# An encoder block in split float32r: branch projections as split products, S5 states turned back before the read-out

## The chip, the cores and the metric

The kernel runs on one core of a Trainium2 chip. The metric is the device time of one execution in microseconds; three timed runs of the kernel before gave 1187.72, 1187.76 and 1188.9, and the median counts. A profiled execution of the same program gives the trace.

## The reference

Two layers over a residual stream x of 256 tokens by 1024 features, all in float32:

```
for l in range(2):
    x = x + 0.5 * swiglu_ffn(rmsnorm(x), ffn1_w_up[l], ffn1_w_down[l])      # hidden width 2816
    h = rmsnorm(x)
    u, q, k, v, z, gates = split(h @ w_in[l])                               # 256, 512, 512, 512, 512, 3072
    y_s5   = GLU(gelu(S5(u)), s5_w_glu[l]) @ w_br_s5[l]     # 16 groups of 16 channels, 64 complex states each
    y_attn = chunked_attention(q, k, v) @ w_br_attn[l]      # 8 heads of 64, chunks of 64
    y_conv = silu(layernorm(conv31(glu(z)))) @ w_br_conv[l] # depthwise, causal, 256 channels
    g = sigmoid(gates + b)
    x = x + (g_s5 * y_s5 + g_attn * y_attn + g_conv * y_conv) @ w_out[l]
    x = x + 0.5 * swiglu_ffn(rmsnorm(x), ffn2_w_up[l], ffn2_w_down[l])
```

S5 is a linear recurrence of complex states, s[t] = a s[t-1] + B u[t] with a = mag e^(i theta), and its output is the real part of C s[t], plus a skip term.

## The kernel before

The residual stream is kept with features on the partitions and 256 tokens along the free dimension, so a weight matrix is used in 128x128 tiles as the stationary operand and a product's moving operand has 256 columns. The tiles come in the order of their use (`PLAN`), eight to a chunk of 512 KB, from one stream of DMAs on SP's queue. For most products (*split* products here) a chunk lands in `raw` (three buffers), ScalarE (ACT) casts it to float32r as `hi`, and VectorE (DVE) subtracts to get the rest, `lo` (four buffers each, in `fetch`). The other operand is split in the same way by `split` (a cast on ACT, a subtraction on DVE), and `prod` adds hi x hi, hi x lo and lo x hi in PSUM: three matmuls.

Three weight matrices of each layer are named in `NATIVE`: `w_br_conv` (16 tiles), `s5_w_glu` (8) and `w_br_s5` (16), five chunks. They land in a `lo` buffer as they are, are not split, and `prod` issues one plain float32 matmul with an operand that isn't split either: the convolution's result `cv`, the GELU's result `gh` (written by `s5_gelu`) and the GLU's result `so` (in buffer `u`).

S5 works in a rotating frame, so that the recurrence becomes a real scan. For each of eight blocks of 128 states, `s5_states` multiplies B u by tables of cos and sin, adds and subtracts, scans twice (real and imaginary part, buffer `sa`), and then multiplies the scans by cos (result `mc`) and by sin (result written over the tables, `tbl`). The four combinations are left apart: for four blocks at a time the read-out on TensorE (PE) adds four products per block, `mc` real and imaginary, `tbl` imaginary and real, with `cc`, which holds C times a coefficient in three forms of sign. These products have a stationary tile of 32 columns, so four sit side by side in the array.

The order of issue is not that of the code. The program is recorded, and a list scheduler (`Recorder.schedule`) runs it with rough prices and puts each engine's instructions in an order that then stands: engines run in order. Among instructions that are ready it takes the lowest rank. The weight stream, products and evacuations have rank 0, the heads of the attention 1, the convolution 2, S5's states and GELU 3, the next layer's S5 tables 4; a matmul of a rank above 0 goes ahead of the others on PE when it is ready. The matrices come in this order: w_in's gates (24 blocks), w_br_attn, four blocks of w_br_conv, s5_w_glu, the other four of w_br_conv, w_br_s5, w_out. The steps of the branches fill in between the gates' products. A block of a branch's projection is multiplied by its gate and added by DVE as it leaves PSUM (two operations for the convolution, two and a split for S5). `w_out` starts with a pair of output blocks that takes its last operand block as late as it can.

Every recorded instruction is issued in one place, so the trace has line 268 for nearly all of them; tiles tell them apart. The prices that the scheduler uses are:

```
return max(n / 2400.0 * (4 * rows / P if slow else 1) + 0.0025, 0.03), 0.2     # PE, n columns
return SLACK * (0.068 + scal + n / (1920.0 if fast else 960.0)), 0.16          # DVE, SLACK = 1.02
```

Of the kernel before, what the change touches and what calls it, by code (L numbers as in the profile page):

```python
"""Two layers of a parallel-branch encoder block (SwiGLU / S5 + attention + conv mixer / SwiGLU).

The residual stream is kept feature-major: x[feature on partitions, feature block, token].
Every large product runs on the tensor engine in float32r: both operands are split exactly
into a high part of 12 significant bits and the remainder, and three products carry the sum.
RMSNorm's 1/rms factor is per token and linear, so it is applied where a product leaves PSUM.
"""
# [10 lines left out]
F32 = mybir.dt.float32  # L18
# [11 lines left out]
CW = 31  # L30
U0, Q0, K0, V0, Z0, G0 = 0, 2, 6, 10, 14, 18     # 128-column blocks of w_in
CHT = 8                                            # weight tiles per DMA
MAGIC = 12582912.0                                 # 1.5 * 2**23: adding it rounds to integers
TWO_PI = 6.283185307179586
C1 = float(np.float32(6.28125))                    # 2*pi in three parts
# [13 lines left out]
GLU = 4                                            # blocks of the convolution's branch ahead of S5's GLU  # L49


def plan():
    out = []
    for l in range(L):
        for f in ("ffn1", "ffn2"):
# [5 lines left out]
            # the last operand block as late as possible  # L61
# [17 lines left out]
NATIVE = ("w_br_conv", "s5_w_glu", "w_br_s5")      # few columns: float32 products, operands not split  # L79
# [20 lines left out]
#  # L100
# The program is first recorded in its logical order. Each engine runs its instructions in the order
# of issue, so that order is then chosen by a list scheduler with rough costs (they depend on shapes
# alone): the weight stream and what frees PSUM go first, the mixer's branches fill in.
# [23 lines left out]
class Recorder:  # L127
# [65 lines left out]
    def price(eng, name, outs, ins, kw):  # L193
# [5 lines left out]
        if eng == "pe":  # L199
            if name == "transpose":  # L200
                return 0.112, 0.2
            slow = kw["rhs"].dtype != F32R or n < 256
            rows = outs[0].partition_size()            # tiles of 32 or 64 columns run side by side
            return max(n / 2400.0 * (4 * rows / P if slow else 1) + 0.0025, 0.03), 0.2
# [12 lines left out]
    def schedule(self):  # L217
# [4 lines left out]
        wait = {e: [] for e in engs}       # (ready time, seq, op)  # L222
        can = {e: [] for e in engs}        # (rank, seq, op)
# [6 lines left out]
        while left:  # L230
# [11 lines left out]
            if soon:                       # a short chain that others wait for: no long one in between  # L242
                free[e] = min(soon)
                continue
# [26 lines left out]
# blocks of x that are loaded ahead of a part (chunk, column) of the weights  # L271
# [8 lines left out]
class Builder:  # L280
# [15 lines left out]
    # -- small helpers --  # L296
# [4 lines left out]
    # Tiles of one tag take turns in their slots, so work that runs at its own pace has its own tags.  # L301
# [15 lines left out]
    # -- weight stream --  # L317
    def fetch(self, upto):
        nc = self.nc
        while self.fetched <= min(upto, NCH - 1):  # L320
            c = self.fetched
            n = min(CHT, len(PLAN) - c * CHT) * P
            if PLAN[c * CHT][1] in NATIVE:
                raw = self.tile(self.chunk, [P, CHT * P], F32, "lo", 4)
                nc.sync.dma_start(out=raw, in_=self.w_d[c])
                self.chunks[c] = (raw, None)
                self.fetched += 1
                continue
# [14 lines left out]
    def wt(self, key, n=1):  # L343
        i = INDEX[key]
        c, o = divmod(i, CHT)
        self.fetch(c + 2)
        hi, lo = self.chunks[c]
        s = slice(o * P, (o + n) * P)
        return hi[:, s], None if lo is None else lo[:, s]

    # -- products: out[feature, token] += w.T @ x --
    def prod(self, out, keys, ops, ks, start, stop):
        nc = self.nc
        for n, k in enumerate(ks):
            wh, wl = self.wt(keys(k))
            if wl is None:
                nc.tensor.matmul(out, lhsT=wh, rhs=ops[:, k, :], start=start and n == 0,
                                 stop=stop and n == len(ks) - 1)
                continue
            if not isinstance(ops, tuple):  # L360
                # one pass over both parts; the halves of out are added where it leaves PSUM
# [18 lines left out]
    def quad(self, outs, l, name, cs, ops, nk):  # L380
        """Output blocks that share every operand block as it arrives."""
        for k in range(nk):
            for o, c in zip(outs, cs):
                self.block(o, l, name, c, ops, nk, k, k + 1)

    def pair(self, outs, l, name, cs, ops, nk):
        """Two output blocks whose last operand block is used as late as possible."""
# [5 lines left out]
    # -- 1/sqrt on a small tile: bit-level seed and three Newton steps --  # L393
# [12 lines left out]
    def col_rsqrt(self, terms, inv_n, eps=EPS):  # L406
        """terms: [feature, token] tiles whose squares' sums over all features give the variance."""
# [10 lines left out]
    def spread(self, rc, out):  # L418
        """out[:, token] = rc[token] on every partition."""
# [9 lines left out]
    # -- RMSNorm: operands x*g split in two, 1/rms per token --  # L429
# [33 lines left out]
    # -- SwiGLU half step --  # L463
# [58 lines left out]
    # -- S5: decay and rotation tables --  # L522
# [23 lines left out]
    def s5_tables(self, l):  # L546
        """Returns a list of steps: cos/sin(theta*s) for every state and s, decay, and C times coef."""
# [7 lines left out]
        def small_part():  # L555
# [4 lines left out]
            # B, for products of split operands stacked along the contraction: rows (hi, hi, lo)  # L560
# [35 lines left out]
        def angle(j):  # L596
            # fraction of a turn in [-1/2, 1/2]
# [21 lines left out]
        def coefs():  # L619
# [17 lines left out]
            # C times coef, with the signs under which the four products of a state add up  # L637
            c4 = st["ct"].rearrange("p (j r c) -> p j r c", j=8, r=2)
            cc = self.tile(self.res, [P, 8, 3, 32], F32, "cc")
# [5 lines left out]
            ts(out=cc[:, :, 1, :], in0=cc[:, :, 0, :], scalar1=-1.0, scalar2=None, op0=ALU.mult)  # L645
            tt(out=cc[:, :, 2, :], in0=c4[:, :, 0, :], in1=b(ci), op=ALU.mult)
            tt(out=t2, in0=c4[:, :, 1, :], in1=b(cr), op=ALU.mult)
            stt(out=cc[:, :, 2, :], in0=cc[:, :, 2, :], scalar=-1.0, in1=t2, op0=ALU.mult, op1=ALU.subtract)
# [5 lines left out]
    # -- mixer --  # L654
    def mixer(self, l, after):
# [6 lines left out]
        # u  # L662
# [12 lines left out]
        # S5 states, two groups (128 states) at a time  # L675
        y_ps = {}

        def s5_states(j):
            if j % 4 == 0:
                # channels of one state block on the same partitions, parts (hi, lo, hi) stacked  # L680
# [27 lines left out]
            # the products with sin take the place of this block's tables  # L708
            mc = self.tmp("mc", 2 * T)
            tt(out=v3(mc), in0=v3(z), in1=b3(cosj), op=ALU.mult)  # L710
            tt(out=tab, in0=v3(z), in1=b3(sinj), op=ALU.mult)
            mcs.append(mc)
            if j % 4 == 3:
# [4 lines left out]
                for n, (w, i) in enumerate(((0, 0), (2, 1), (1, 1), (2, 0))):  # L718
                    for q in range(4):
                        jj = 4 * b + q  # L720
                        rhs = (mcs[jj][:, i * T:(i + 1) * T] if n < 2 else st["tab"][:, jj, i, :])
                        nc.tensor.matmul(y_ps[0][32 * q:32 * q + 32, b * T:(b + 1) * T], lhsT=cc[:, jj, w, :], rhs=rhs,
                                         start=n == 0, stop=n == 3, tile_position=(0, 32 * q))
# [4 lines left out]
        def s5_gelu(b):  # L728
            # gelu(y) (tanh form), doubled
# [8 lines left out]
            if not ge:  # L738
                ge["y"] = self.tile(self.big, [P, 2, T], F32, "gh")
            stt(out=ge["y"][:, b, :], in0=t, scalar=1.0, in1=y, op0=ALU.add, op1=ALU.mult)  # L740

        # conv: GLU with both halves of z
# [13 lines left out]
        # q, k, v with tokens on partitions  # L756
# [23 lines left out]
        # operands of the gates: normalised, in place  # L780
# [5 lines left out]
        # twice the convolution (hp holds twice the GLU): LayerNorm takes that out, with four times EPS  # L786
# [3 lines left out]
        cv = self.tile(self.big, [P, 2, T], F32, "cv")  # L790

# [11 lines left out]
        def conv_norm():  # L803
# [17 lines left out]
            for q in range(2):  # L821
                # silu(v), doubled: v*(1 + tanh(v/2))
# [4 lines left out]
                stt(out=cv[:, q, :], in0=th, scalar=1.0, in1=v, op0=ALU.add, op1=ALU.mult)  # L827
# [71 lines left out]
        # gates, with the branches' steps in between  # L899
# [19 lines left out]
        # branches' projections, gated and added  # L919
# [5 lines left out]
        def conv_block(j):  # L925
            ps = self.bank(("mm", "at", "mm", "at", "mm")[j % 5])
            self.block(ps[:, :T], l, "w_br_conv", j, cv, 2)
# [6 lines left out]
        so = self.tile(self.big, [P, 2, T], F32, "u")  # L934
        for b in range(2):
# [5 lines left out]
            stt(out=so[:, b, :], in0=t, scalar=1.0, in1=ps[:, :T], op0=ALU.add, op1=ALU.mult)  # L941
# [30 lines left out]
    def warm_up(self):  # L972
        """While the first loads are under way: the tensor engine's clock up, the Tanh table in."""
# [11 lines left out]
    def build(self):  # L985
        nc = self.nc
        # small parameters of the first layer and x come as one array
# [33 lines left out]
def layout(inputs):  # L1021
# [8 lines left out]
    sb = np.zeros((L, 3, 2, 16, 8, 2, 2, 64), np.float32)      # copy, g, ch | jb, re/im, g, state  # L1030
    for l in range(L):
# [19 lines left out]
        ct = np.zeros((2, 64, 8, 2, 2, 16), np.float32)        # g, state | jb, re/im, g, ch  # L1051
# [7 lines left out]
    # relative position bias per head, blocks (q 0..127, k 0..127) and (q 128..255, k 0..255);  # L1059
    # keys of later chunks are masked  # L1060
# [3 lines left out]
    full = inp["attn_rel_bias"][:, :, rel]                     # L, heads, q, k  # L1064
# [29 lines left out]
```

## Time and profile before

| | us |
|---|---|
| timed runs, median (three runs) | 1187.76 (1187.72 to 1188.9) |
| profiled execution: span from the first to the last instruction | 1186.6 |
| what the runs' median has on top of that span | 1.2 |
| PE busy | 1177.4 |
| PE weight loads (beside PE) | 1097.8 |
| DVE busy | 927.2 |
| ACT busy | 645.6 |

The profiled execution is given by its span; no time of its own from outside is listed beside it, so the runs' median stands for it. Busy is the union of an engine's instructions. A matmul's record is longer than the distance to the next, since matmuls overlap; that distance, from start to start, is called pitch below, and it is what a product costs on a full PE. The granted clock of PE is full (1.000 of 2.4 GHz) over the whole span.

### The profile page before, as it was taken

The page shows a single profiled execution, that of the slowest core. Times are in us where ns is not written, and L with a number is a line of the kernel's source. Part 1 is how long each engine was busy: PE and PEld are TensorE (multiplying, and loading weights), DVE is VectorE, ACT ScalarE, POOL GpSimd, SP SyncE. Part 2 cuts the span into 40 slices and gives each one's busy share as a digit, 9 for nine tenths or more (in the row PEclk, how much of TensorE's full clock was granted, in tenths as well). Part 3 has the DMA queues.
Part 4 walks back from the last instruction along what each step waited for, and adds up shares of the span by engine and source line. Part 5 has one row for each costly group of instructions (what it writes and reads, how often), then busy time and mean ns, then how long its engine had stood idle before and what let it go on. Part 6 is the DMA issues. An engine that isn't in the chain of part 4 may idle for free.

```text
span 1186.6 us, 21932 instructions
## 1 busy us (share of the span) xinstructions
PE 1177.4 (99%) x8565; PEld 1097.8 (93%) x8565; DVE 927.2 (78%) x1898; ACT 645.6 (54%) x1171; POOL 13.0 (1%) x32
## 2 busy tenths in 40 slices
PE   8999999999999999999999999999999999999998
PEld 7999989898888999998899999898987999999987
DVE  7999876998789998766676666779987888666654
ACT  6546554787643546645544444557875435444442
POOL 0000000000200000000000000000001000000000
PEclk9999999999999999999999999999999999999999
DMA  7655556554334565555555555565533435555552
GB/s 253 212 181 187 195 182 226 195 178 146 101 131 162 178 196 187 187 178 191 182 178 186 187 179 190 184 213 198 192 126 94 152 126 194 194 179 182 189 198 89
DMA packets 59751, 209.97 MB, mean 177 GB/s; under 512 B 6912, under 2 KB 9088, under 8 KB 59392
## 3 DMA queue, kind: packets, MB, share of 16 engines
q1 hardware_dynamic: 58496, 207.79, 50.9%
q8 instruction: 67, 1.10, 0.4%
q0 software_dynamic: 1152, 0.79, 0.3%
q14 instruction: 36, 0.29, 0.1%
HBM read 206.72 MB, written 1.05 MB: 175 GB/s over the span
## 4 chain that ended last, share of the span: by engine, by line
PE 98%; DMA 1%; DVE 0%; ACT 0%; SPq 0%; issue 0%; DVEq 0%
PE mm L268 72%; PE at L268 22%; PE ax L268 2%; PE y L268 1%; DMA px<-in_x 1%; PE pq L268 0%; SPq L268 0%; DVE x L268 0%; DVE acc L268 0%; ACT sq L268 0%; DVE lo L268 0%; DVE ev L268 0%; ACT x L268 0%; DVE px L268 0%; ACT ev L268 0%
## 5 line engine op out<-in xcount | busy, mean ns | idle before, releaser
L268 ACT CAST hi<-raw 128x1024 fp32r<-128x1024 f32 (+1 forms) x373 | 389.8, 1047 | 406.8 <-issue 166.7
L268 DVE TENSOR_TENSOR lo<-raw,hi 128x1024 fp32r<-128x1024 f32 (+1 forms) x373 | 454.9, 1221 | 165.7 <-ACT hi L268 161.9
L268 PE MATMUL mm<-x,hi 128*128 128x256 f32 x2736 | 505.8, 284 | 1.9 <-ACT hi L268 1.8
L268 PEld LDWEIGHTS mm<-x,hi 128*128 128x128 f32 x2736 | 424.5, 189 | 11.4 <-issue 7.4
L268 PE MATMUL mm<-x,lo 128*128 128x256 f32 x1368 | 388.3, 285 | 0.4 <-DVE lo L268 0.2
L268 PEld LDWEIGHTS mm<-x,lo 128*128 128x128 f32 x1368 | 257.2, 188 | 4.7 <-issue 3.8
L268 PE MATMUL mm<-AB,hi 128*128 128x512 f32 x704 | 246.6, 398 | 0.0
L268 PE MATMUL mm<-AB,lo 128*128 128x256 f32 x704 | 193.1, 281 | 0.0
L268 PE MATMUL at<-x,hi 128*128 128x256 f32 x1040 | 188.6, 282 | 0.1
L268 PEld LDWEIGHTS at<-x,hi 128*128 128x128 f32 x1040 | 160.6, 189 | 0.3 <-ACT hi L268 0.3
L268 PEld LDWEIGHTS mm<-AB,hi 128*128 128x128 f32 x704 | 130.6, 188 | 29.7
L268 PE MATMUL at<-x,lo 128*128 128x256 f32 x520 | 146.6, 282 | 0.0
L268 PEld LDWEIGHTS mm<-AB,lo 128*128 128x128 f32 x704 | 132.9, 189 | 2.6
L268 PEld LDWEIGHTS at<-x,lo 128*128 128x128 f32 x520 | 97.9, 188 | 0.0
L268 PE MATMUL mm<-tbl,hi 128*128 128x256 f32 x256 | 46.3, 284 | 0.0
L268 PE MATMUL at<-hi,x 128*128 128x512 f32 x128 | 41.0, 396 | 0.0
L268 PEld LDWEIGHTS mm<-tbl,hi 128*128 128x128 f32 x256 | 39.9, 192 | 0.3 <-ACT tbl L268 0.3
L268 ACT ACTIVATE th<-ev 128x256 f32<-128x256 f32 x88 | 36.2, 412 | 7.2 <-DVE ev L268 7.0
L268 ACT CAST AB<-ev 128x256 fp32r<-128x256 f32 x88 | 34.9, 400 | 6.5 <-DVE ev L268 6.2
L268 DVE SCALAR_TENSOR_TENSOR ev<-th,ev 128x256 f32<-128x256 f32 x88 | 36.8, 419 | 1.2 <-ACT th L268 1.2
L268 DVE TENSOR_TENSOR AB<-ev,AB 128x256 fp32r<-128x256 f32 x88 | 36.6, 419 | 0.4 <-ACT AB L268 0.2
L268 DVE TENSOR_TENSOR ev<-mm,rb 128x256 f32<-128x256 f32 x56 | 23.6, 424 | 15.6 <-PE mm L268 13.5
(222 smaller groups left out, 1174.1 us busy)
## 6 DMA issues: line engine op xcount, KB each, us to landing
raw<-in_w SPq DMA_DIRECT2D x371, 512.0 KB, 3.7
lo<-in_w SPq DMA_DIRECT2D x10, 512.0 KB, 4.4
AB<-in_b SPq DMA_DIRECT2D x2, 1536.0 KB, 7.9
mc<-in_s SPq DMA_DIRECT2D x8, 192.0 KB, 4.1
out_x<-px SPq DMA_DIRECT2D x8, 128.0 KB, 3.2
raw<-in_w SPq DMA_DIRECT2D x2, 256.0 KB, 3.8
px<-in_x SPq DMA_DIRECT2D x1, 512.0 KB, 7.7
ct<-in_p SPq DMA_DIRECT2D x2, 256.0 KB, 3.7
```

Of the source, the lines that this page charges most:

```text
L268: fn(*args, **kw)
```

## The change

The three matrices of `NATIVE` go through the same way as all others: their chunks land in `raw`, are cast and split, and the products have three float32r matmuls. Their operands are split where they are written: the convolution's result into `cv2`, which takes the buffers of `ct` and `hp`; the GELU's into the buffers `gh` and `gl`; the GLU's into the buffer `us`. And in S5 two more operations per block (`mc` real minus `tbl` imaginary, `mc` imaginary plus `tbl` real) turn the states back, so that the read-out has two products per block in place of four and `cc` two forms in place of three. Comments that go are left out here.

```diff
-NATIVE = ("w_br_conv", "s5_w_glu", "w_br_s5")      # few columns: float32 products, operands not split
 def fetch(self, upto):
...
-            if PLAN[c * CHT][1] in NATIVE:
-                raw = self.tile(self.chunk, [P, CHT * P], F32, "lo", 4)
-                nc.sync.dma_start(out=raw, in_=self.w_d[c])
-                self.chunks[c] = (raw, None)
-                self.fetched += 1
-                continue
 def prod(self, out, keys, ops, ks, start, stop):
...
-            if wl is None:
-                nc.tensor.matmul(out, lhsT=wh, rhs=ops[:, k, :], start=start and n == 0,
-                                 stop=stop and n == len(ks) - 1)
-                continue
 # s5_tables, coefs
-            cc = self.tile(self.res, [P, 8, 3, 32], F32, "cc")
+            cc = self.tile(self.res, [P, 8, 2, 32], F32, "cc")
-            ts(out=cc[:, :, 1, :], in0=cc[:, :, 0, :], scalar1=-1.0, scalar2=None, op0=ALU.mult)
 # s5_states
             tt(out=v3(mc), in0=v3(z), in1=b3(cosj), op=ALU.mult)
             tt(out=tab, in0=v3(z), in1=b3(sinj), op=ALU.mult)
+            tt(out=mc[:, :T], in0=mc[:, :T], in1=tab[:, 1, :], op=ALU.subtract)
+            tt(out=mc[:, T:], in0=mc[:, T:], in1=tab[:, 0, :], op=ALU.add)
...
-                for n, (w, i) in enumerate(((0, 0), (2, 1), (1, 1), (2, 0))):
+                for r in range(2):
                     for q in range(4):
                         jj = 4 * b + q
-                        rhs = (mcs[jj][:, i * T:(i + 1) * T] if n < 2 else st["tab"][:, jj, i, :])
-                        nc.tensor.matmul(y_ps[0][32 * q:32 * q + 32, b * T:(b + 1) * T], lhsT=cc[:, jj, w, :], rhs=rhs,
-                                         start=n == 0, stop=n == 3, tile_position=(0, 32 * q))
+                        nc.tensor.matmul(y_ps[0][32 * q:32 * q + 32, b * T:(b + 1) * T], lhsT=cc[:, jj, r, :],
+                                         rhs=mcs[jj][:, r * T:(r + 1) * T], start=r == 0, stop=r == 1,
+                                         tile_position=(0, 32 * q))
 # s5_gelu
-                ge["y"] = self.tile(self.big, [P, 2, T], F32, "gh")
-            stt(out=ge["y"][:, b, :], in0=t, scalar=1.0, in1=y, op0=ALU.add, op1=ALU.mult)
+                ge["y"] = tuple(self.tile(self.big, [P, 2, T], F32R, g) for g in ("gh", "gl"))
+            stt(out=t, in0=t, scalar=1.0, in1=y, op0=ALU.add, op1=ALU.mult)
+            self.split(t, ge["y"][0][:, b, :], ge["y"][1][:, b, :])
 # mixer
+        cv2 = (self.tile(self.big, [P, 2, T], F32R, "ct"), self.tile(self.big, [P, 2, CW - 1 + T], F32R, "hp")[:, :, :T])
 # conv_norm
-                stt(out=cv[:, q, :], in0=th, scalar=1.0, in1=v, op0=ALU.add, op1=ALU.mult)
+                stt(out=v, in0=th, scalar=1.0, in1=v, op0=ALU.add, op1=ALU.mult)
+                self.split(v, cv2[0][:, q, :], cv2[1][:, q, :])
 # conv_block
-            self.block(ps[:, :T], l, "w_br_conv", j, cv, 2)
+            self.block(ps[:, :T], l, "w_br_conv", j, cv2, 2)
 # mixer, S5's GLU
-        so = self.tile(self.big, [P, 2, T], F32, "u")
+        so = self.tile(self.big, [P, 2, 2, T], F32R, "us")
+        so = (so[:, 0, :, :], so[:, 1, :, :])
...
-            stt(out=so[:, b, :], in0=t, scalar=1.0, in1=ps[:, :T], op0=ALU.add, op1=ALU.mult)
+            stt(out=t, in0=t, scalar=1.0, in1=ps[:, :T], op0=ALU.add, op1=ALU.mult)
+            self.split(t, so[0][:, b, :], so[1][:, b, :])
```

## Rows read from the trace of the kernel before

**Rows 1.** The page, part 1: busy us (share of the span) xinstructions of each engine.

```profile
PE 1177.4 (99%) x8565; PEld 1097.8 (93%) x8565; DVE 927.2 (78%) x1898; ACT 645.6 (54%) x1171; POOL 13.0 (1%) x32
```

**Rows 2.** The page, part 4: the chain that ended last, by engine.

```profile
PE 98%; DMA 1%; DVE 0%; ACT 0%; SPq 0%; issue 0%; DVEq 0%
```

**Rows 3.** Windows: length, busy us of each engine, clock, DMA share, GB/s, of six stretches.

```profile
251.50:351.70 100.20, 100.20 (x761) 88.34 (x760) 85.08 (x202) 64.22 (x158) 5.96 (x12) 1.00 0.39 131
351.70:369.60 17.90, 17.90 (x144) 16.32 (x144) 14.65 (x38) 9.60 (x16) 0.00 (x0) 1.00 0.65 218
369.60:383.10 13.50, 13.50 (x64) 11.64 (x62) 13.31 (x31) 3.44 (x7) 0.00 (x0) 1.00 0.35 119
383.10:389.60 6.50, 6.50 (x55) 6.50 (x55) 6.50 (x16) 1.55 (x4) 0.00 (x0) 1.00 0.21 79
837.20:937.60 100.40, 100.40 (x760) 88.39 (x759) 84.83 (x198) 64.43 (x158) 5.81 (x12) 1.00 0.38 131
937.60:952.90 15.30, 15.30 (x134) 14.04 (x133) 12.68 (x34) 7.42 (x12) 0.00 (x0) 1.00 0.51 172
```

**Rows 4.** Chain in order of time, FFN1 of layer 0: start us, us, what.

```profile
33.75 17.28 PE mm L268 x144
```

**Rows 5.** Timeline of PE, projections of layer 0: start us, us, engine, instruction, count.

```profile
365.73 1.03 PE L268 MATMUL mm<-cv,lo 128*128 128x256 f32 x4
...
369.18 3.62 PE L268 MATMUL mm<-gh,lo 128*128 128x256 f32 x16
372.64 1.89 PE L268 MATMUL mm<-cv,lo 128*128 128x256 f32 x8
```

**Rows 6.** Timeline of PE around one single read-out product, layer 0.

```profile
341.42 0.27 PE L268 MATMUL mm<-x,hi 128*128 128x256 f32 x1
341.63 0.62 PE L268 MATMUL y<-mc,cc 128*32 128x256 f32 x2
...
342.40 0.28 PE L268 MATMUL mm<-x,lo 128*128 128x256 f32 x1
```

**Rows 7.** Timeline of PE around the second group of read-out products, layer 0.

```profile
361.89 0.28 PE L268 MATMUL mm<-nat,hi 128*128 128x256 f32 x1
362.10 0.83 PE L268 MATMUL y<-mc,cc 128*32 128x256 f32 x9
...
362.78 1.24 PE L268 MATMUL y<-tbl,cc 128*32 128x256 f32 x13
...
364.17 0.28 PE L268 MATMUL mm<-nat,lo 128*128 128x256 f32 x1
```

**Rows 8.** Timeline of DVE, layer 0, behind the GLU and in the first output pair.

```profile
373.91 0.42 DVE L268 SCALAR_TENSOR_TENSOR u<-ev,mm 128x256 f32<-128x256 f32 x1
...
388.00 1.22 DVE L268 TENSOR_TENSOR lo<-raw,hi 128x1024 fp32r<-128x1024 f32 x1
389.14 0.42 DVE L268 TENSOR_TENSOR tbl<-ev,tbl 128x256 fp32r<-128x256 f32 x1
389.47 0.35 DVE L268 TENSOR_SCALAR sa<-iota,fh 128x256 f32<-128x256 f32 x1
```

**Rows 9.** Waits of DVE in the gates of layer 0: us, times, longest.

```profile
DVE lo L268 <- ACT hi L268: 7.0, 12, 1.4
```

**Rows 10.** Timeline of DVE around the GELU's last write, layer 0, then layer 1.

```profile
366.79 0.42 DVE L268 SCALAR_TENSOR_TENSOR ev<-AB,mm 128x256 f32<-128x256 f32 x1 [0.24 <-PE mm L268]
...
369.14 0.42 DVE L268 SCALAR_TENSOR_TENSOR gh<-sc,sa 128x256 f32<-128x256 f32 x1
369.47 0.42 DVE L268 SCALAR_TENSOR_TENSOR AB<-ev,AB 128x256 f32<-128x256 f32 x1
...
952.45 0.43 DVE L268 SCALAR_TENSOR_TENSOR gh<-sc,sa 128x256 f32<-128x256 f32 x1
952.86 0.42 DVE L268 SCALAR_TENSOR_TENSOR ev<-AB,mm 128x256 f32<-128x256 f32 x1
```

**Rows 11.** The page, part 6: DMA issues, count, KB each, us to landing.

```profile
raw<-in_w SPq DMA_DIRECT2D x371, 512.0 KB, 3.7
```

More of the change, by code (lines that the diff above doesn't have):

```diff
@@ L348, in wt @@
         s = slice(o * P, (o + n) * P)
-        return hi[:, s], None if lo is None else lo[:, s]
+        return hi[:, s], lo[:, s]
     def prod(self, out, keys, ops, ks, start, stop):
@@ L644, in coefs @@
             tt(out=cc[:, :, 0, :], in0=cc[:, :, 0, :], in1=t2, op=ALU.subtract)
-            ts(out=cc[:, :, 1, :], in0=cc[:, :, 0, :], scalar1=-1.0, scalar2=None, op0=ALU.mult)
-            tt(out=cc[:, :, 2, :], in0=c4[:, :, 0, :], in1=b(ci), op=ALU.mult)
+            tt(out=cc[:, :, 1, :], in0=c4[:, :, 0, :], in1=b(ci), op=ALU.mult)
             tt(out=t2, in0=c4[:, :, 1, :], in1=b(cr), op=ALU.mult)
-            stt(out=cc[:, :, 2, :], in0=cc[:, :, 2, :], scalar=-1.0, in1=t2, op0=ALU.mult, op1=ALU.subtract)
+            stt(out=cc[:, :, 1, :], in0=cc[:, :, 1, :], scalar=-1.0, in1=t2, op0=ALU.mult, op1=ALU.subtract)
             st["cc"] = cc
```

## The prediction

> **What bounds the kernel now.** I read the page first, then the chain, then the stages, then single instructions. The page shows TensorE (PE) busy for 1177.4 of 1186.6 us [rows 1], and the chain that ended last is PE for 98% [rows 2]. Where PE never stops, the time is the sum of the pitches (start to start) of its matmuls, so a cheaper product would be worth its whole saving. But that is a mean over stages. The table by stage [rows 3] has one line for each stretch around the change: the gates with S5, heads and convolution in between (251.5 to 351.7 and 837.2 to 937.6), the start of the attention projection up to the write of S5's GELU (351.7 to 369.6, 937.6 to 952.9), the rest of the projections (369.6 to 383.1) and the first output pair. PE is busy all through, and VectorE (DVE) is 85% busy in the gates (85.08 of 100.20), 82 and 83% ahead of the GELU, 99% behind it (13.31 of 13.50), 100% after that. So in the second half of the mixer DVE has almost nothing to spare, and the first question is whether PE or DVE sets the end there.
>
> **What PE saves.** A split matmul of 256 columns has a pitch of 0.120 us (17.28/144) [rows 4], three of them 0.36. A plain float32 product is two instructions in the trace: 16 of them, eight products, take 372.64 - 369.18 = 3.46 us [rows 5], 0.4325 each. The change turns 2 layers x (16 + 8 + 16) products: 80 x (0.4325 - 0.36) = 5.8 us. The read-out goes from 64 products to 32. One alone costs 342.40 - 341.42 - 2 x 0.12 = 0.74 us [rows 6]; a group of 13 (26 instructions, two rows left out) costs 364.17 - 361.89 - 0.24 = 2.04 [rows 7], so each further one (2.04 - 0.74)/12 = 0.108. The scheduler issues the first three state blocks' products singly and the rest as a group, and what goes are eight from each of four groups: 32 x 0.108 = 3.5 us. Bounds: 3.5 if all lie in groups, 23.7 (32 x 0.74) if all were single; I take 3.5, since the products that stand alone are first products, which stay. PE's work falls by 9.3 us, 4.65 a layer.
>
> **What DVE gets.** From successive rows, a split of a weight chunk has a pitch of 1.14 us (389.14 - 388.00) and a tensor_tensor of 128x256 one of 0.33 (389.47 - 389.14) [rows 8]. Per layer: five more chunks are split (two of w_br_conv, one of s5_w_glu, two of w_br_s5), 5.7 us; two more operations turn each of eight states back, 16 x 0.33 = 5.3; six splits (cv2, GELU, so), 2.0. One sign change in the tables goes, in a stage with slack: nothing. Together 13.0 us a layer on an engine that is full in the stages behind the GELU. ScalarE gets five casts of a chunk and six of 128x256, but is busy only 64% in the gates and 54% in the next stretch: nothing, as long as DVE is later.
>
> **How much of it is hidden.** In the gates DVE has 15.1 us idle, most of it (7.0) waiting for the cast of a weight chunk [rows 9], which waits for a buffer that PE frees. The DVE queue is in order, and that order was chosen by the list scheduler with its own prices: 256/2400 + 0.0025 = 0.109 us for a PE matmul (the trace: 0.120), and 1.02 x (0.068 + 256/960) = 0.341 for a DVE operation (the trace: 0.33). So by its prices the gates last some 91 us and DVE fills 85.1 x 1.02 = 87 of them: about 4 us look free to it, though 15 are free on the chip. S5 has the lowest rank there. Rotations of seven blocks, 14 x 0.33 = 4.6 us, fall into the gates; between 0 and 4.6 of it, or of the work that it displaces, runs over into the next stage. I take 3.5, since chains of heads and states use some of the 4 us already.
>
> **The stretch up to S5's GLU.** DVE's work that must be done before the GLU's operands are there: 14.65 and 12.68 us of before [rows 3]; the overrun 3.5; the last block's rotation, cv2 and GELU splits, 6 x 0.33 = 2.0; three chunks (convolution twice, GLU) 3.4; and the gated adds of the convolution's blocks. PE will find the GLU not ready and the scheduler, which takes what is ready, puts all eight blocks first; their 16 adds have rank 0 and go ahead of the GELU's rank. In layer 0 six of them are in the window (366.79 to 369.47), in layer 1 none (the first at 952.86) [rows 10]: 10 x 0.33 = 3.3 and 16 x 0.33 = 5.3 more. Sum 26.9 us in both layers. PE has from the same start 14.0 us up to the first convolution product at 365.73 [rows 5] (layer 1 is taken alike) less 0.9 for the smaller read-out group, plus 16 x 0.36 = 5.8: 18.9. So PE stands about 8 us at the GLU, in each layer. This was without slack before: the GELU's last write ran from 369.14 to 369.56 [rows 10], the GLU's first product started at 369.18 [rows 5] and its second weight block at 369.61.
>
> **Behind the GLU.** GLU 8 x 0.36 = 2.9; then PE waits for `so`, since the convolution blocks no longer stand in between: before, its last write ended at 374.33 [rows 8], 1.7 us behind the GLU's last product; with the cast ahead I take 1.9. Then w_br_s5 16 x 0.36 = 5.8. Together 10.5. The three DVE operations of each of its blocks, 8 x 1.0 = 8.0 us, and two chunk splits (2.3) end 10.3 us after w_br_s5 starts; w_out's first pair reads the last block 5.8 + 14 x 0.36 = 10.8 us after it: hidden, with half a microsecond to spare.
>
> **The sum.** 26.9 + 10.5 = 37.4 us a layer, against 383.1 - 351.7 = 31.4 before: 6.0 longer; the first read-out group in the gates gives back 0.9. Two layers: +10.3 us. The span of 1186.6 becomes 1196.9; the runs' median lies 1.2 above that span, so 1198.
>
> **Kept at nothing.** The ten chunks now land in `raw`, three buffers, in place of `lo`, four. Transfers took 3.7 us [rows 11] against 2.9 us of PE per chunk with three in flight, as everywhere else in the kernel; without that cover 0.8 us a chunk, 8 in all. The next layer's `ct` load on SP's queue now waits for the last convolution product (it shares the buffer with cv2); weights are queued behind it, and if it were issued early they would come late by a few us, once.
>
> **Rivals.** *The change is hidden* (faster): the rotations fill DVE's idle time in the gates and the GELU is done in time; PE stays the bound. Then 1187.8 - 9.3 = 1178.5. For it: 15 us idle in the gates and 2.6 to 3.3 in the next stretch. Against: the scheduler does not see most of it. It decides if DVE gets 8 of these us a layer; partly, it gives 1180 to 1185. *Even*: overrun 0 and one chunk later: 5.1 - 3.5 - 1.1 = +0.5 a layer, 1189. *Worse packing*: overrun 4.6, a fourth chunk (w_br_s5) ahead of the GELU, and the 2.9 us a layer that DVE idled here before in the chain through ScalarE and PE stay: +5.1 a layer more, 1208. *Evacuation sets the pace in w_br_s5*: a block costs PE 0.72 us and DVE 1.0, and if the w_out pair doesn't cover it, the difference of 2.2 us and the two splits, 4.5 a layer, are added: 1207; against it, the 0.5 us to spare above. The Trainium skill, TensorEngine Tiling, section PSUM Bottleneck, warns of just that: a faster TensorE does not speed up the copies out of PSUM, which may become the limit, and ScalarE and VectorE should share them; here DVE alone does them, and no row of before shows which way it goes.
>
> **How the numbers follow.** Hidden 0.21, even 0.08, my forecast (1190 to 1204, its own range) 0.51, worse packing 0.13, evacuation 0.07. A difference under 0.2% (2.4 us) can't be told from none here. Faster is 0.21, the same 0.08, slower 0.71. For 8 in 10 the range reaches down to the hidden case, 1179, and up to 1206, which leaves about 0.06 below and 0.13 above.
>
> **What would show it.** In the profile after: split matmuls in place of cv,lo, gh,lo and u,lo at a pitch of 0.12; 64 y instructions in place of 128; in each layer a gap of some 8 us on PE ahead of the GLU, released by DVE, and one of about 2 behind it; DVE near 100% from the attention projection on. If PE has no gap there, I am wrong about the overrun and the kernel is faster; if DVE is idle while PE waits, it is the chain's latency and not DVE's work.

## The result

The changed kernel takes 1223.96 us (median of four runs, 1223.5 to 1224.25) against 1187.74 (four runs, 1187.37 to 1188.9): a ratio of 1.0302, 95% interval 1.0287 to 1.0316. That is 36.2 us slower, where 10.3 were forecast: the direction is as predicted, the time lies far above the range (1179 to 1206). The profiled execution has a span of 1221.8 us.

The page after, part 1 (busy time of each engine) and from part 4 the chain that ended last, by engine:

```profile
PE 1181.5 (97%) x8581; PEld 1104.2 (90%) x8581; DVE 954.0 (78%) x1950; ACT 660.3 (54%) x1193; POOL 12.9 (1%) x32
...
PE 93%; DVE 4%; DMA 1%; ACT 1%; issue 1%; SPq 0%; DVEq 0%; ACTq 0%
```

PE is no longer busy all through: the chain was PE for 98% [rows 2] and is now for 93%, with DVE in its place. The windows after, by stage: the gates of layer 0, from the first attention product to the GLU's first product, from there to `w_out`'s first product, two stretches of five and ten us inside these, and the two tail stages of layer 1 (columns as in [rows 3]):

```profile
250.88:347.97 97.09, 97.09 (x740) 87.50 (x738) 82.67 (x196) 64.28 (x158) 5.94 (x12) 1.00 0.42 135
347.97:382.96 34.99, 23.50 (x152) 19.59 (x150) 30.57 (x71) 11.33 (x19) 0.00 (x0) 0.78 0.39 128
382.96:400.35 17.39, 13.11 (x85) 11.94 (x85) 16.15 (x41) 8.62 (x16) 0.00 (x0) 0.86 0.17 50
365.00:370.00 5.00, 4.78 (x19) 3.45 (x18) 4.16 (x11) 0.40 (x1) 0.00 (x0) 0.50 0.28 97
375.00:385.00 10.00, 3.76 (x17) 2.10 (x18) 7.97 (x20) 4.21 (x10) 0.00 (x0) 0.50 0.35 124
...
953.02:987.40 34.38, 22.36 (x152) 18.53 (x150) 30.19 (x68) 10.72 (x17) 0.00 (x0) 0.87 0.32 108
987.40:1003.91 16.51, 12.86 (x84) 12.28 (x85) 11.29 (x29) 7.20 (x13) 0.00 (x0) 0.86 0.12 34
```

Layer 0 against the forecast: the gates are 3.1 us shorter than before (100.20 to 97.09; forecast 0.9), the stretch up to the GLU is 35.0 us long (forecast 26.9), the one behind it 17.4 (forecast 10.5). 35.0 + 17.4 - 31.4 - 3.1 = 17.9 us for the layer, where 5.1 were forecast. Layer 1, from its first gate product to `w_out`'s first (837.18 to 968.88 us before, 855.93 to 1003.91 after), takes 16.3 us longer in the same places; the small rest of the 36.2 lies outside these stages. The waits of PE in the tail of layer 0, which had none before (us in total, times, longest):

```profile
PE y L267 <- DVE mc L267: 5.4, 1, 5.4
PE mm L267 <- ACT gh L267: 3.4, 1, 3.4
PE mm L267 <- ACT ct L267: 2.4, 2, 2.2
PE mm L267 <- DVE ev L267: 2.3, 1, 2.3
PE mm L267 <- DVE us L267: 0.8, 1, 0.8
PE mm L267 <- DVE gl L267: 0.6, 2, 0.4
PE mm L267 <- ACT us L267: 0.6, 1, 0.6
PE mm L267 <- DVE hp L267: 0.3, 1, 0.3
```

They come to 15.8 us, in layer 1 (950 to 1010) to 15.6: 31.4 together. Where they stand is seen in the timeline of PE (the bracket is the idle time before the row and what ended it):

```profile
363.22 0.38 PE L267 MATMUL mm<-ct,hi 128*128 128x256 f32 x1 [2.19 <-ACT ct L267]
...
364.63 0.42 PE L267 MATMUL mm<-ct,lo 128*128 128x256 f32 x1
364.85 0.41 PE L267 MATMUL at<-hp,hi 128*128 128x256 f32 x1
...
377.67 1.92 PE L267 MATMUL y<-mc,cc 128*32 128x256 f32 x10 [5.41 <-DVE mc L267]
382.96 0.79 PE L267 MATMUL mm<-gh,hi 128*128 128x256 f32 x2 [3.38 <-ACT gh L267]
...
388.00 0.28 PE L267 MATMUL mm<-gh,lo 128*128 128x256 f32 x1
388.12 0.28 PE L267 MATMUL mm<-gh,hi 128*128 128x256 f32 x1
...
400.35 0.47 PE L267 MATMUL mm<-tbl,hi 128*128 128x256 f32 x2 [2.25 <-DVE ev L267]
```

First the convolution's operand comes late, then the last read-out group waits for the last block's states, then the GLU for the GELU, and at the end `w_out` for an evacuation. A split matmul has its pitch of 0.12 us at full clock (388.00 to 388.12), but 0.21 where the granted clock is 0.50 of 2.4 GHz (364.63 to 364.85; the window rows 365 to 370 and 375 to 385): the clock falls behind the waits. Counted from PE, layer 0's 52.4 us are 15.8 of waits, about 29.1 of matmuls at full clock (18.9 + 2.9 + 5.8 of the forecast, and two single read-out products, 2 x 0.74, which now come after the gates), and 7.5 more; layer 1's 50.9 are 15.6, the same 29.1, and 6.2 more. Less the 9.3 us saved on PE that gives 31.4 + 13.7 - 9.3 = 35.8, against 36.2 measured. Not all of the 13.7 goes with the clock: by the pitches some 10 us of it (an estimate) are matmuls at the half clock, and the rest stands beside the waits, where a matmul's record of 0.28 us counts whole and not its pitch.

Three other rows answer to those of before, from the timeline, the waits of DVE in the gates and the DMA issues:

```profile
331.21 1.05 PE L267 MATMUL y<-mc,cc 128*32 128x256 f32 x10
```

```profile
DVE lo L267 <- ACT hi L267: 6.2, 13, 0.9
```

```profile
raw<-in_w SPq DMA_DIRECT2D x381, 512.0 KB, 3.9
```

Five read-out products in a group take about a microsecond, as priced from [rows 7]; DVE waits in the gates for casts nearly as long as before, 6.2 us against 7.0 [rows 9]: the time that was free is still free. The ten chunks more in `raw` land in 3.9 us, against 3.7 [rows 11].

What DVE does ahead of the GLU, from its timeline: the state work of block 5 to 7 that is still to be done when the attention projection starts, first and last rows, and the wait that follows.

```profile
348.18 0.69 DVE L267 TENSOR_TENSOR sc<-pq,tbl 128x512 f32<-128x512 f32 x1
...
361.73 0.68 DVE L267 TENSOR_TENSOR_SCAN sa<-mag,sa 128x256 f32<-128x256 f32 x1
...
377.19 0.76 DVE L267 TENSOR_TENSOR mc<-mc,tbl 128x256 f32<-128x256 f32 x2
379.62 0.87 DVE L267 SCALAR_TENSOR_TENSOR sa<-u,px,y 128x256 f32<-128x256 f32 x2 [1.67 <-PE y L267]
```

The stretch holds 11 operations of 512 columns or scans at a pitch of 0.60 and 10 of 256 at 0.33 of this kind, 9.9 us. Before, it held 3.1: two of 0.33, and the two scans and two products of 0.60 that these rows show:

```profile
358.81 1.27 DVE L268 TENSOR_TENSOR_SCAN sa<-mag,sa 128x256 f32<-128x256 f32 x2
...
360.30 0.69 DVE L268 TENSOR_TENSOR mc<-sa,tbl 128x512 f32<-128x512 f32 x1
...
361.02 0.69 DVE L268 TENSOR_TENSOR tbl<-sa,tbl 128x512 f32<-128x512 f32 x1
```

### The profile page after: what moved, and what is told of

Same layout as the page of the kernel before. It is cut to its first block, busy times and chain, and to the rows that moved or that the text cites. A ratio compares the mean times of both kernels' runs of the same rounds, so it can differ in the third digit from the quotient of the medians.

```text
span 1221.8 us, 22052 instructions
## 1 busy us (share of the span) xinstructions
PE 1181.5 (97%) x8581; PEld 1104.2 (90%) x8581; DVE 954.0 (78%) x1950; ACT 660.3 (54%) x1193; POOL 12.9 (1%) x32
## 3 DMA queue, kind: packets, MB, share of 16 engines
HBM read 206.72 MB, written 1.05 MB: 170 GB/s over the span
## 4 chain that ended last, share of the span: by engine, by line
PE 93%; DVE 4%; DMA 1%; ACT 1%; issue 1%; SPq 0%; DVEq 0%; ACTq 0%
PE mm L267 69%; PE at L267 21%; PE ax L267 2%; PE y L267 1%; DMA raw<-in_w 1%; DVE lo L267 1%; DVE ev L267 1%; ACT hi L267 1%; DVE sa L267 0%; DVE AB L267 0%; PE pq L267 0%; DVE cv L267 0%; DVE mc L267 0%; DVE sc L267 0%; DVE tbl L267 0%
## 5 line engine op out<-in xcount | busy, mean ns | idle before, releaser
L267 ACT CAST hi<-raw 128x1024 fp32r<-128x1024 f32 (+1 forms) x383 | 400.3, 1047 | 422.6 <-PE mm L267 187.0
L267 DVE TENSOR_TENSOR lo<-raw,hi 128x1024 fp32r<-128x1024 f32 (+1 forms) x383 | 466.9, 1220 | 166.6 <-ACT hi L267 163.6
L267 ACT ACTIVATE th<-ev 128x256 f32<-128x256 f32 x88 | 36.2, 412 | 7.1 <-DVE ev L267 7.0
L267 PE MATMUL mm<-tbl,lo 128*128 128x256 f32 x128 | 36.7, 289 | 0.0
```

The source lines that it names most:

```text
L267: fn(*args, **kw)
```

## The experiments

Three theories were tested. **Theory 1:** the loss is DVE's added work in the mixer, which is late there and makes PE wait. **Theory 2:** it is PE's clock, halved behind the waits, that makes the tail long. **Theory 3:** the order is what puts the work in the tail: the scheduler prices a PE matmul at 0.109 us in place of 0.120 and so doesn't see DVE's free time in the gates. Theories 1 and 3 can both hold.

**The states alone.** The kernel before, with the rotation and the read-out of two products; `NATIVE` stays.

```diff
...
             tt(out=tab, in0=v3(z), in1=b3(sinj), op=ALU.mult)
+            tt(out=mc[:, :T], in0=mc[:, :T], in1=tab[:, 1, :], op=ALU.subtract)
+            tt(out=mc[:, T:], in0=mc[:, T:], in1=tab[:, 0, :], op=ALU.add)
...
```

> The kernel before with S5's states turned back and read out by two products, nothing else; the five chunks stay plain float32. It adds 16 tensor_tensor of 128x256 a layer to DVE (5.3 us) and takes 1.75 us a layer from PE. Theory 1 (DVE work in the mixer's second half sets the end, and PE waits for it; 26 us of added DVE work cost 36 + 9 = 45 us of PE's time, 1.75 each): 1187.7 + 1.75 x 10.7 - 3.5 = about 1203, with PE waiting ahead of S5's GLU in each layer. Rival A (the rotations are absorbed in the gates, the weight splits alone are to blame): 1184, no wait.

Measured: 1203.04 us (1202.59 to 1205.29), ratio 1.0134 (1.0119 to 1.0149), as theory 1 expected (its price of 1.75 was taken from the changed kernel's own result). PE's two longest waits in layer 0:

```profile
PE y L268 <- DVE mc L268: 3.0, 1, 3.0
PE mm L268 <- DVE gh L268: 2.8, 1, 2.8
```

So 5.3 us of DVE work a layer already break the cover that [rows 10] showed to be without slack: the read-out waits for the rotated states, the GLU for the GELU.

**The split alone.** The kernel after, without the rotation and with four products per block.

```diff
-            tt(out=mc[:, :T], in0=mc[:, :T], in1=tab[:, 1, :], op=ALU.subtract)
-            tt(out=mc[:, T:], in0=mc[:, T:], in1=tab[:, 0, :], op=ALU.add)
...
-                for r in range(2):
+                for n, (w, i) in enumerate(((0, 0), (2, 1), (1, 1), (2, 0))):
...
```

> The changed kernel with the four read-out products of before and no rotation: only the branch projections are split. It adds five chunk splits and six operand splits a layer to DVE (7.7 us) and takes 2.9 us from PE. Theory 1 with the same price for DVE work: 1187.7 + 1.75 x 15.4 - 5.8 = about 1209. Rival A: as slow as the changed kernel, 1224 less 3.5 at the most. Rival B (the two parts only hurt together, one alone fits into DVE's idle time): 1182.

Measured: 1209.38 us (1208.3 to 1211.97), ratio 1.0187 (1.0171 to 1.0202). The two parts, +15.0 and +21.4 us, add up to 36.4, the whole change is 36.2: neither part hides or feeds the other.

**The split without its subtraction.** The kernel after; for the ten chunks DVE's subtraction is left out.

```diff
-            lo = self.tile(self.chunk, [P, CHT * P], F32R, "lo", 4)
+            bare = PLAN[c * CHT][1] in ("w_br_conv", "s5_w_glu", "w_br_s5")
+            lo = hi if bare else self.tile(self.chunk, [P, CHT * P], F32R, "lo", 4)
...
+                if not bare:
...
```

> The changed kernel without DVE's subtraction for the five chunks of each layer: their lo tile is the cast's result, so the products are as many but the third of each is of the wrong tile. Takes 5.7 us of work a layer from DVE and nothing from PE. Theory 1: 1224 - 1.75 x 11.4 = about 1204; at one us for one, 1212.6. Rival C (the wait is the chain's latency and the order of issue, not the amount of DVE work): 1220 to 1224.

Measured: 1207.34 us (1206.12 to 1208.25), ratio 1.0163 (1.0146 to 1.018). 10 x 1.14 = 11.4 us of DVE work less make the kernel 16.6 us faster: each microsecond was worth 1.46, not the one that the forecast charges.

**None of the added DVE work.** As the last one, and without the rotation and the six splits a layer of the operands.

```diff
-            tt(out=mc[:, :T], in0=mc[:, :T], in1=tab[:, 1, :], op=ALU.subtract)
-            tt(out=mc[:, T:], in0=mc[:, T:], in1=tab[:, 0, :], op=ALU.add)
...
-            self.split(t, so[0][:, b, :], so[1][:, b, :])
...
```

> The changed kernel without any of the added DVE work: no rotation, the lo tile of the five chunks and the lo part of the three operands are the high parts, which DVE writes as before. The products are as many as in the changed kernel, on wrong data. This is the case in which PE is the bound: by the pitches 1187.9 - 9.3 = 1178.6. If it is well above, PE still waits for something else than the added DVE work (the convolution blocks no longer cover the GLU, evacuation in w_br_s5): up to 1190.

Measured: 1188.08 us (ten runs, 1185.98 to 1190.41), ratio 1.0002 (0.9993 to 1.0011). PE has the changed, cheaper matmuls here and DVE no more to do than before (926.8 us busy, 927.2 before), and yet the saving of 9.3 us doesn't show. ScalarE's six casts a layer of these operands go with their splits, so the chain to the GLU is one cast shorter than in the kernel after; the run doesn't part the two. The waits of PE, layer 0 (layer 1 has the second alone, 2.4 us):

```profile
PE mm L267 <- DVE gh L267: 2.7, 1, 2.7
PE mm L267 <- DVE ev L267: 2.7, 1, 2.7
```

and a window of five us behind each of them, where the granted clock is lower:

```profile
370.00:375.00 5.00, 4.75 (x28) 4.75 (x29) 4.33 (x12) 1.46 (x4) 0.00 (x0) 0.68 0.07 26
...
385.00:390.00 5.00, 5.00 (x31) 5.00 (x31) 5.00 (x12) 1.48 (x4) 0.00 (x0) 0.66 0.32 103
```

The shorter projections uncover the GELU and the evacuation, which the slower float32 products had covered; these 7.8 us of waits are most of the 9.3. (1223.96 - 1188.08)/26.0 us of DVE work is 1.4 per microsecond, as above.

**PE kept at work.** The kernel after, with 110 matmuls a layer of the lowest rank that PE does when nothing else is ready; nothing reads them.

```diff
...
+        self.rank(9)
+        warm = self.bank("ax")
+        for i in range(110):
+            nc.tensor.matmul(warm[:, :T], lhsT=self.xh[:, 0, :P], rhs=self.xh[:, i % KD, :], start=True, stop=True)
```

> The changed kernel with 110 more float32r matmuls of 256 columns in each layer, of the lowest rank, into a bank that nobody reads: the scheduler puts them where PE has nothing to do, that is ahead of the GLU. They cost PE 13 us a layer at full clock and read data that is there. In the changed kernel PE's clock is granted at half in much of the mixer's tail, while it waits. Theory 2 (the half clock behind each wait is a good part of the loss, some 6 us a layer): the clock stays at 1.0 up to the GLU and the time falls by 6 to 12 us, to 1212 to 1218. Theory 1 alone (PE waits for DVE, so its clock doesn't matter): 1224, or some us more where the fillers come in the way.

Measured: 1225.49 us (1224.96 to 1226.39), ratio 1.032 (1.0304 to 1.0335). A window of layer 0, and PE's and DVE's rows around the read-out:

```profile
360.00:380.00 20.00, 19.92 (x165) 18.57 (x163) 16.61 (x38) 3.42 (x5) 0.00 (x0) 1.00 0.26 87
```

```profile
372.66 6.27 PE L267 MATMUL ax<-x 128*128 128x256 f32 x51
378.87 1.05 PE L267 MATMUL y<-mc,cc 128*32 128x256 f32 x10
383.50 0.50 PE L267 MATMUL mm<-gh,hi 128*128 128x256 f32 x2 [3.58 <-ACT gh L267]
```

```profile
376.87 0.76 DVE L267 TENSOR_TENSOR mc<-mc,tbl 128x256 f32<-128x256 f32 x2
```

The clock is full up to 380 us, the convolution has its short pitch, and the GLU still starts at 383.50 (382.96 without the fill). Up to the read-out the half clock costs next to nothing: DVE starts the last states' rotation at 376.87 in place of 377.19, and PE only waits longer for it. Theory 2 falls for that stretch. In the read-out this run doesn't decide: the group took 1.05 us in place of 1.92, but started at 378.87 in place of 377.67, since 51 of the fillers stood ahead of it on PE.

**A fill between read-out and GLU**, 26 matmuls in bank `y`, for the clock behind the GLU's wait.

```diff
...
+        self.rank(9)
+        warm = self.bank("y")
+        for i in range(26):
...
```

> The changed kernel with 26 more lowest-rank matmuls of 256 columns in each layer that can start once the GELU has read the read-out's bank, so that they fill PE's wait between the read-out and the GLU. Theory 2b (the half clock counts where PE itself is on the chain, in the 24 GLU products that followed at a pitch of 0.21): the GLU runs at full clock and 2 to 3 us a layer are won, 1218 to 1220. Without an effect of the clock: 1224.

Measured: 1223.47 us (1222.62 to 1225.08), ratio 1.0301 (1.0285 to 1.0316): no difference to the kernel after that can be told. The timeline shows why it decides nothing:

```profile
380.52 4.93 PE L267 MATMUL y<-x 128*128 128x256 f32 x26 [1.06 <-DVE sa L267]
385.29 0.40 PE L267 MATMUL mm<-gh,hi 128*128 128x256 f32 x2
```

The 26 ran at 0.19 us each, most of them at half clock themselves, and the GLU started 2.3 us later than without them (385.29, not 382.96); it then ran at 0.12 and ended at about 388.1, against 388.8. What the half clock costs in the read-out and the GLU stays open. At the most it is what the pitches give, an estimate: 0.9 us a layer in the read-out group and about 1.9 in the GLU, under 6 us in both layers.

**The price of a PE matmul.** The kernel after; only the scheduler's price changes, from 0.109 to the 0.120 us of [rows 4], and with it the order.

```diff
-            return max(n / 2400.0 * (4 * rows / P if slow else 1) + 0.0025, 0.03), 0.2
+            return max(n / 2400.0 * (4 * rows / P if slow else 1) + 0.0133, 0.03), 0.2
```

> The changed kernel with one constant of the list scheduler changed: 0.0133 in place of 0.0025 in PE's price, so that a 256-column matmul has the 0.120 us of the trace and not 0.109. No instruction is added or removed, only their order changes. Theory 3 (the scheduler takes DVE for full in the gates, where it is idle 15% of the time on the chip, and leaves S5's blocks for the tail): S5 ends earlier by its prices, the waits at the read-out and the GLU shrink to less than half, 1195 to 1207. If DVE's work itself is too much for the mixer, the order doesn't help: 1220 to 1224.

Measured: 1198.55 us (1197.37 to 1200.43), ratio 1.0091 (1.0076 to 1.0106): 25.4 us faster than the kernel after, with the same instructions. The same 94 us of the gates in the kernel after and in this one, and PE's two longest waits in the tail of layer 0:

```profile
251.00:345.00 94.00, 94.00 (x715) 84.41 (x714) 79.88 (x190) 62.74 (x156) 5.94 (x12) 1.00 0.42 134
251.00:345.00 94.00, 94.00 (x696) 82.29 (x694) 84.07 (x206) 61.78 (x151) 5.96 (x12) 1.00 0.40 130
```

```profile
PE mm L267 <- DVE gl L267: 2.6, 2, 1.8
PE mm L267 <- DVE ev L267: 1.9, 1, 1.9
```

DVE does 84.07 us of work in the same 94 us in which it did 79.88 in the kernel after; the first read-out group is issued at 319.35 in place of 331.21, and the wait of 5.4 us for the last states is gone. Theory 3 holds: 25.4 of the 36.2 us hang on the order. The price changes the whole order, and no run parts S5's earlier end from the rest of it.

**The states alone, with that price; the kernel before, with that price.** The same line changed in the first experiment's kernel and in the kernel before.

> The kernel before with the states turned back (as e1_states_only) and PE's price in the scheduler at 0.0133, as in e8_price. Theory 3 (with a price that fits the trace the rotations go into DVE's idle time in the gates): the 15 us that e1 lost come back and the 3.5 us of PE's smaller read-out show: 1187.9 - 3.5 = 1184.4, faster than before. If rotations can't be hidden even so: 1190 to 1200.

> The kernel before with that price and nothing else, as the measure for the run beside it. PE never waits in the kernel before, so a better order has nothing to win: 1187.9, within 0.2%. If the price itself helped (fewer switches between tile shapes, say), e9's gain would not be the read-out's.

Measured, 11 runs each: the states 1185.45 us (1184.08 to 1186.49), ratio 0.9976 (0.9967 to 0.9985); the kernel before 1191.05 (1189.97 to 1192.18), ratio 1.0026 (1.0017 to 1.0034). The first is faster than both kernels of the case. PE has no wait in its mixer, the mean granted clock is 1.000, and DVE takes the rotations into the gates, 90.15 us of 100.20 against 85.08 [rows 3]:

```profile
251.50:351.70 100.20, 100.20 (x751) 88.83 (x751) 90.15 (x217) 65.44 (x157) 5.97 (x12) 1.00 0.41 131
```

With the same price the read-out of two products is 5.6 us better than that of four, against 3.5 forecast on PE; beside the kernel before as it stands it is 2.6. Alone, the price makes the kernel before 3.0 us slower, which was not expected: counted in the timeline, PE goes over to the form of 32 columns 24 times in place of 20, and at 0.74 - 0.11 = 0.63 us each [rows 6, 7] that would be 2.5 us. With two products and that price it is 18 times, which would be 3.8 of the 5.6 us. That is worked out and not tested.

**The work on GpSimd.** The kernel after, with the rotations and the subtraction of the ten chunks on GpSimd; then the same with the new price.

```diff
...
-                nc.vector.tensor_tensor(out=lo[:, a:b], in0=raw[:, a:b], in1=hi[:, a:b].bitcast(F32),
-                                        op=ALU.subtract)
+                e = nc.gpsimd if PLAN[c * CHT][1] in ("w_br_conv", "s5_w_glu", "w_br_s5") else nc.vector
+                e.tensor_tensor(out=lo[:, a:b], in0=raw[:, a:b], in1=hi[:, a:b].bitcast(F32), op=ALU.subtract)
...
```

> The changed kernel with the rotations of the states and the subtraction for the five chunks of each layer on GpSimd in place of DVE (the operand splits stay on DVE); the scheduler is given a guess of 0.84 us for 128x256 and 2.8 us for 128x1024 there. It takes 11.0 of the 13.0 us a layer off DVE, and no PE work. Theory 1 (what counts is the amount of work on DVE): most of the 45 us that PE waited goes, to 1185 to 1195. Rival C (the length of the chain counts: GpSimd's operations are slower and a further engine stands in it): 1205 or more.

> The changed kernel with the rotations and the five chunks' subtraction on GpSimd (as e5_pool) and the price of e8_price. e5 stayed at 1224.5, with waits for GpSimd's results and DVE operations that were stretched while GpSimd ran. If the order was most of e5's trouble: below e8's 1198.5, some 1185 to 1192. If GpSimd's own pace and what it does to DVE is the trouble: no better than e8, 1198 to 1210.

Measured: 1224.5 us (1222.76 to 1225.09), ratio 1.0303 (1.0286 to 1.032), no gain; with the price 1196.18 (1195.58 to 1196.93), ratio 1.0069 (1.0053 to 1.0084), 2.4 us better than the price alone and short of what was expected. GpSimd's groups in the first of the two, and two of its operations beside two rows of DVE:

```profile
L269 POOL TENSOR_TENSOR mc<-mc,tbl 128x256 f32<-128x256 f32 x32 | 26.6, 848 | 879.4 <-ACT AB L269 520.6 <-DVE mx L269 300.6 <-DVE tbl L269 38.4
L269 POOL TENSOR_TENSOR lo<-raw,hi 128x1024 fp32r<-128x1024 f32 x10 | 24.9, 2494 | 19.5 <-ACT hi L269 15.9 <-DVE ev L269 3.6
```

```profile
354.86 2.65 POOL L269 TENSOR_TENSOR lo<-raw,hi 128x1024 fp32r<-128x1024 f32 x1 [2.24 <-ACT hi L269]
358.48 2.77 POOL L269 TENSOR_TENSOR lo<-raw,hi 128x1024 fp32r<-128x1024 f32 x1 [0.97 <-ACT hi L269]
```

```profile
355.18 2.35 DVE L269 SCALAR_TENSOR_TENSOR nt<-nt,v 128x2 f32<-128x2 f32 x1
...
359.03 2.49 DVE L269 TENSOR_SCALAR sq<-ident,y 128x128 f32<-128x128 f32 x2
```

A DVE operation on 128x2, which takes 0.15 us elsewhere, ran for 2.35 us, until GpSimd's subtraction ended (354.86 + 2.65 = 357.51; 355.18 + 2.35 = 357.53). The pair of `sq`, 0.48 us before, ran for 2.49. The work moved off DVE comes back as longer operations there: on the page DVE is busy for 961.3 us, 954.0 in the kernel after, though 22.0 us of work left it. The Trainium skill, SBUF — State Buffer, section SBUF: two separate sides, says that a DVE operation with two inputs in SBUF and a GpSimd operation that reads SBUF block each other for the whole instruction; the row of `nt`, which has two inputs, agrees.

**Other banks for the last pair.** The kernel after; `w_out`'s first pair goes to the banks `y` and `pq`, which are free, in place of two of `mm`.

```diff
-        p2 = [self.bank(), self.bank()]
+        p2 = [self.bank("y"), self.bank("pq")]
```

> The changed kernel with w_out's first pair in the PSUM banks of the read-out and of S5's states (idle by then) in place of two of the three that w_br_s5's blocks share. In the changed kernel, and in e6_all_off too, PE waits 2.3 to 2.7 us a layer ahead of w_out, released by the DVE operation that empties a bank. Rival 'evacuation sets the pace in w_br_s5': if the banks are what PE waits for, that wait goes and up to 4.5 us are won, 1219 to 1221. If it is w_out's operand that is late, as the prediction's sum assumed, the wait moves into w_out's first pair and the time stays at 1224.

Measured: 1220.1 us (1219.31 to 1220.31), ratio 1.0266 (1.0249 to 1.0284): 3.9 us faster, as expected. The wait of 2.3 us ahead of `w_out` is gone in both layers; half a microsecond for the `lo` of a weight chunk is left in its place:

```profile
PE mm L267 <- DVE lo L267: 0.5, 1, 0.5
```

PE waited there for a PSUM bank that DVE had not emptied yet, not for an operand.

## Why the prediction was wrong

**Right.** The direction, and where it would be seen: 64 `y` instructions, split products at 0.12, a gap of PE ahead of the GLU behind DVE (8 us forecast; 5.4 + 3.4 there), one or two more behind it. DVE's added work is the cause, in the order that the scheduler gave it: the parts add up, without that work (and the six casts a layer) the loss is gone, and with another order most of it is gone.

**How much of it is hidden: the step that failed.** The overrun was taken as 3.5 us, at most 4.6, the rotations of seven blocks. It was 9.9 - 3.1 less the 0.7 of the last block's own rotation, which was counted apart: 6.1. The bound was none, because it assumed that DVE does at least its old work in the gates. It did less: 82.67 us against 85.08 [rows 3]. The gates ended 2.2 us earlier than assumed, and the idle time in them stayed unused (14.4 us; 15.1 before). The mispricing of 0.109 against 0.120 was named in this step, but taken as a limit on what could be gained, not as what makes the tail long. With the right price the same instructions are 25.4 us faster; with the rotation alone and that price PE has no wait in the mixer. In layer 0 the forecast is missed by 12.8 us: 8.1 up to the GLU and 6.9 behind it, less these 2.2. The overrun's own size is 2.6 of them; the rest is in the next two steps, which failed too.

**The stretch up to the GLU** was summed as DVE's work without idle time, 26.9. DVE worked for 30.6 (the overrun is 2.6 of the difference) and stood still for 4.4, of which 1.7 while PE did the read-out that it waited for: it was 87% busy, not near 100% as the prediction would see it. The chain from the last states over read-out, GELU and cast to the GLU has nothing beside it any more, and such a chain costs its latency on all engines. The convolution's operand, another 2.2 us late, was not foreseen. That may be why a microsecond of DVE work cost 1.4 and not one; it is argued from these rows, and no run takes the price apart.

**Behind the GLU** 10.5 became 17.4. The GLU took 5.9 (382.96 to 388.83) in place of 2.9, with 0.6 of waits and a pitch of 0.21 in much of it: the forecast had no clock below full. Two of the eight convolution blocks came after it, not all before: 12 x 0.12 = 1.4. The evacuation, "hidden, with half a microsecond to spare", took 2.3 more. The waits for `so` were 1.4 in place of 1.9. That is 3.0 + 1.4 + 2.3 - 0.5 = 6.2 of the 6.9; the rest is not placed. The last experiment shows that the spare half microsecond was figured for the wrong thing: the operand may be in time, but the pair also needs banks that the same slow evacuation frees. The rule of the Trainium skill (TensorEngine Tiling (Array Packing), section PSUM Bottleneck) that the prediction weighed, with 0.07, held: 2.0 us a layer of the 4.5 that this rival was priced at.

**The rivals.** They were taken as alternatives, but worse packing and evacuation came together, and with a halved clock. So the range's upper end was too low. And the hidden case, 1178.5, could not be had in the order of these prices: with no added DVE work at all the time is 1188.08. A saving of PE in a place where PE covers a chain of DVE and ACT is only worth the slack of that chain, and the prediction had noted that there was none. Whether the corrected price would give that slack was not run; for the states alone it did.

**Open:** the half clock's share in the read-out and the GLU, and the 3.0 us that the price costs the kernel before.

## What to carry to other kernels

Before work is moved to a helper engine, look in the stage where it lands at that engine's busy share, and at whether the order (a queue that somebody's prices wrote) can reach its idle time; free time in a window of the profile is not free if the order was made with prices that hide it, and prices taken from the trace can be worth more than the change. A shorter product on the bound engine pays only as far as the chains that it covered are shorter too, so sum the chain's latency over all engines, not the busy time of one. Cases that one late engine causes come together: add their prices before setting the upper end of a range.

## What the hardware showed that was not expected

- Behind most of the waits of 2 to 5 us PE's granted clock fell to 0.50 (1.2 GHz), and a split matmul's pitch was 0.21 us in place of 0.12; behind the wait of 2.25 us ahead of layer 1's `w_out` it stayed at 1.00. Keeping PE at work up to the read-out held the clock at 1.00 there, and the last states were ready only 0.3 us earlier, as DVE set the time.
- GpSimd took 0.85 us for a tensor_tensor of 128x256 and 2.49 for 128x1024 (DVE's pitches: 0.33 and 1.14), and DVE's operations beside it were held up: one of 0.15 us took 2.35 and ended with GpSimd's.
